# A hybrid decoder layer on one core: another order for the steps of a half's mix, and other PSUM banks for two units

## The chip, the cores and the metric

The kernel runs on one core of one Trainium2 chip. The metric is the device time of one execution in microseconds. Three runs of the kernel before gave 2166.95, 2167.82 and 2168.07 us; their median, 2167.82 us, is the time before.

The engines are TensorE (PE in the profile, its weight loads are PEld), VectorE (DVE), ScalarE (ACT), GpSimd (POOL) and SyncE (SP, which here issues DMAs). Matmul results go to PSUM, which has eight banks of 128 x 512 float32.

## The reference, cut to what matters

One layer of a decoder over 2048 tokens of width 1024 in float32. The input is normalised and projected; four heads of a gated linear recurrence (HGRN2) and eight heads of sliding-window attention with sinks run side by side; their outputs are concatenated, projected by `w_out` and added to the input. A gated MLP with a causal depthwise convolution and a last norm follow.

```python
u = rmsnorm(h, norm_mix_w[l])
proj = u @ w_in[l]
hq, hf, hi, hg, att = jnp.split(proj, [...], axis=-1)
f = lb + (1.0 - lb) * jax.nn.sigmoid(hf)          # forget gate, k = 1 - f
o_hg = hgrn2_chunkwise(q_hg, 1.0 - f, v_hg, jnp.log(f))
o_hg = rmsnorm(o_hg, hg_norm_w[l]) * jax.nn.silu(hg)
o_att = sliding_window_attention_with_sinks(aq, ak, av, sinks[l])
h = h + jnp.concatenate([o_hg, o_att], axis=-1) @ w_out[l]
v = rmsnorm(h, norm_ffn_w[l])
gate = causal_depthwise_conv(v @ w_gate[l], conv_w[l], conv_b[l])
h = h + (jax.nn.silu(gate) * (v @ w_up[l])) @ w_down[l]
```

## The kernel before

**Tiling.** Activations lie transposed: features on the 128 partitions, tokens along the free axis. The tokens are worked in two halves of 1024. Every float32 operand of a large product is split into a high and a low part of type fp32r (`split`, `prep`, lines 186 to 229: a copy on ScalarE and a subtraction on VectorE), and a product is three matmuls: high times high, high times low, low times high. The norm's scale of a token is applied when a result is read out of PSUM.

**A unit** (`unit`, line 195) is the product of a 1024 x 128 weight tile with the half's activations: eight input tiles (`X`, or the finished mix `M`) times three matmuls times two banks of 512 tokens, 48 matmuls into two banks. The weights come by DMA into one of three buffers and are split in a ring of two.

**PSUM.** Line 64 to 66 divide the eight banks: four `mm` for the units, and four side banks, two `hg` and two `at`. `kind="aux"` puts a unit's two results into one `hg` and one `at` bank.

**The mix of a half** (lines 1200 to 1238) works four recurrent heads and four pairs of attention heads. Both are Python generators that give back control between steps. `hgrn` (line 524) has five steps:

- 1: the units of the forget gate (`f`) and the query (`hq`), and their read-out;
- 2: products on the diagonal, then seven levels of doubling block size (`LEVELS`); a level copies operands on ScalarE (`G`, line 601), multiplies on TensorE (`plev`), scales `QK` by `F` on VectorE (line 615) and puts the block into `ST`; levels 2 to 16 send a part round by a small DMA on ScalarE's queue (line 582);
- 3: `pkn`, the state products `pu`, and the running states `SS`;
- 4: the output gate's unit `g`;
- 5: the products `po`, their norm, the transposition `pot`, and the gated output.

For the last head the gate's unit comes in step 2, after the diagonal, and the levels alone are step 3; `pu` is step 4 and the output step 5. `QK`, `f` and `SS` have one buffer each, so a head waits there for the one before it.

`attend` (line 431) has four steps: the query unit `q`; the scores `psc` of both token groups with their softmax; and the weighted sums of group 0 and of group 1 (`ppt` transposes, two masks on VectorE, `poT`).

The output of a head goes to `mix[h]`, of a pair to `mix[4 + j]`. The last head and the last pair write theirs split; the other six are split at lines 1214 and 1215, into the buffers of `X`, which come free as the last unit, the last head's gate, passes over them. `out_proj` (line 744) then runs eight units `pop` over the tiles of `M` in the order 0, 4, 1, 5, 2, 6, 7, 3. `BEHIND` (line 38) puts parts of its second and third unit behind marks of the last head: the third unit's first tile behind `pu`, its third behind `po`, its sixth behind `pot`.

**Between the halves.** `down` (line 1017) runs seven products (a Strassen scheme) over the four `mm` banks and the four side banks in turn. In the first half its last two are P2 in the side banks and P4 in `mm`; VectorE adds them to `hh` (lines 1137 to 1146). It then starts the next half: the keys' unit and the values' unit (`first_unit`, both in `mm`), among which two sums `pst` and their spreads `pinv` (lines 258 to 288) go through the side banks, and the forget gates of the first head, `f0`, in the side banks (lines 1185 to 1187). The first half gets the same three from `head` (line 314).

**What sets the order.** The framework plans the order of instructions ahead, with a simulated clock. The order of the program is the order of priority: each engine takes what is ready, by the simulation, and stands first in the program. So a unit that stands later in the program fills TensorE between the small products of earlier steps. `tc.issue_after` puts an instruction behind another on the same engine. On the chip each engine runs its planned list in order.

In each half, with H for `next` of a recurrent head, A of an attention pair, W and V for the values' weights and product, G for the early split of a gate's weights and S for the six splits, the order before is:

```
H0 A0 W H0 V G0 A0 H0 H0 A0 A0 H0
H1 H1 A1 G1 A1 H1 H1 A1 A1 H1
H2 H2 A2 G2 A2 H2 H2 A2 A2 H2
H3 A3 H3 S H3 A3 H3 A3 H3 A3
```

Of the kernel before, what the change touches and what calls it, by code (L numbers as in the profile page):

```python
# [19 lines left out]
KT = D // P  # L20
S = 2048
# [4 lines left out]
HG = 4  # L26
ATT_J = 4
# [16 lines left out]
WARM = 12  # L44
TAIL_WARM = 7
LV = 4


@with_exitstack
def hymba_layer(ctx: ExitStack, tc: tile.TileContext, a: dict, out: bass.AP):  # L50
    nc = tc.nc

    def pool(name, bufs=1, space=None, stack=ctx, **kw):
        if space is not None:
            kw["space"] = space
        return stack.enter_context(tc.tile_pool(name=name, bufs=bufs, **kw))
# [12 lines left out]
    def ps(kind, name):  # L69
        return spaces[kind].tile([P, 512], F32, tag=kind, name=name)  # L70

    aux = ("hg", "at")

    def halves():
        return [(b, slice(b * 512, (b + 1) * 512)) for b in range(NB)]
# [104 lines left out]
    def raw4(src):  # L180
        t = wp.tile([P, D], F32, tag="raw", name="raw", bufs=RAW)
        if src is not None:
            nc.sync.dma_start(t, src)
        return t

    def prep(src, slots=False):

        raw = raw4(src)
        hi, lo = [hp.tile([P, D], F32R, tag="m", name=f"w{t}", bufs=KT) if slots else
                  wp.tile([P, D], F32R, tag=t, name=f"w{t}", bufs=2) for t in ("hi", "lo")]  # L190
        nc.scalar.copy(hi, raw)  # L191
        nc.vector.tensor_tensor(lo, raw, hi.bitcast(F32), op=ALU.subtract)  # L192
        return hi, lo

    def unit(src, X, name, order=range(KT), kind="mm", then={}, behind={}, in_turn=False):


        hi, lo = src if isinstance(src, tuple) else prep(src)
        o = [ps(aux[b] if kind == "aux" else kind, f"{name}{b}") for b in range(NB)]
        order, mark = list(order), None  # L200
        for both in [[h] for h in halves()] if in_turn else [halves()]:
            for i, kt in enumerate(order):
                if i in then:
                    then[i]()
                wh, wl = hi[:, kt * P:(kt + 1) * P], lo[:, kt * P:(kt + 1) * P]
                xh, xl = X[kt]
                if i in behind:
                    mark = marks[behind[i]].ins
                with tc.issue_after(mark) if mark else ExitStack():
                    for w, x, f, l in ((wh, xh, kt == order[0], False), (wh, xl, False, False),  # L210
                                       (wl, xh, False, kt == order[-1])):
                        for b, bs in both:
                            marks["unit"] = nc.tensor.matmul(o[b], w, x[:, bs], start=f, stop=l)  # L213
        return o
# [5 lines left out]
    def split(src, w=None, eng=None, dst=None):  # L220

        h, l = dst or new_x()
        if w is None:
            nc.scalar.copy(h, src)
            (eng or nc.vector).tensor_tensor(l, src, h.bitcast(F32), op=ALU.subtract)
        else:
            nc.scalar.activation(h, src, AF.Identity, scale=w)
            nc.vector.scalar_tensor_tensor(l, src, w, h.bitcast(F32), op0=ALU.mult, op1=ALU.subtract)
        return h, l
# [161 lines left out]
            f0 = unit(F, X, "f", kind="aux", then={4: st.spread}, behind={4: "pinv"})  # L391
        return o, st.acc, st.rs, f0, summed

    def first_unit(X, i, then={}):
        return unit(a["w_att"][ATT_J + i], X, "kv", then=then)

    def rows(kv):
        return slice(kv * HD, (kv + 1) * HD)
# [125 lines left out]
    def hgrn(hf, h, X, invb, vs, WG, mix, p, fu=None):  # L524
# [51 lines left out]
        def place(m, pl):  # L576

            plv = pl.rearrange("p (r b c m) -> p r b c m", r=R, c=2, m=m)
            moved, odd = [p.tile([P, R, 64], F32, tag="lv", name=n, bufs=LV) for n in ("moved", "odd")]
            nc.scalar.copy(moved.rearrange("p r (b m) -> p r b m", m=m), plv[:, :, :, 1])  # L580
# [118 lines left out]
    def project_v(hf, parts, X, rs, p):  # L699

        v = p.tile([P, HG, TT, P], F32, name="v")
        for tt in range(TT):
            o = ps("mm", "pvv")
            t = slice(tt * P, (tt + 1) * P)
            for kt in range(KT):
                hi, lo = parts[kt // 2]
                xh, xl = X[kt]
                c = slice((kt % 2) * 512, (kt % 2 + 1) * 512)
                nc.tensor.matmul(o, xh[:, t], hi[:, c], start=kt == 0, stop=False)
                nc.tensor.matmul(o, xl[:, t], hi[:, c], start=False, stop=False)  # L710
                nc.tensor.matmul(o, xh[:, t], lo[:, c], start=False, stop=kt == KT - 1)
            nc.scalar.activation(v[:, :, tt], o.rearrange("p (h d) -> p h d", h=HG), AF.Identity,
                                 scale=rs[:, tt:tt + 1])
        return [v[:, h] for h in range(HG)]
# [302 lines left out]
    def down(hf, kept, acts, p):  # L1017
# [8 lines left out]
        S = {}  # L1026
# [78 lines left out]
        X, xs, acc = [], None, None  # L1105
        end = len(todo) - NP
        for k, (name, _, _, j) in enumerate(todo):
            if k + 2 < len(todo):
                ready[k + 2] = prep_piece(k + 2)
            if j == 0:  # L1110
# [4 lines left out]
                else:  # L1115
                    o = by if name == "P3" else bx
                if name == "P3":
                    acc = inv_tile() if final else wp.tile([P, HALF], F32, tag="raw", name="sums", bufs=RAW)
                    s1, s2 = [Stats(acc[:, bs], lambda: p.tile([P, 512], F32, tag="ut", name="fsq", bufs=UT))
                              for bs in (lo, hi)]  # L1120
# [3 lines left out]
            if not final and k >= end - 3:  # L1124
                xs = next(loading, xs)
# [29 lines left out]
        if final:  # L1155
# [26 lines left out]
            steps[1][0].inverse("o", last)  # L1182
            finish(hf, hh, steps[1][0], steps[1][1], [nc.scalar, nc.sync], steps[1][0].spread(1))
            return None
        kv = [first_unit(X, 0, {3: lambda: s1.inverse("o"), 7: lambda: xs.inverse("x")})]
        kv.append(first_unit(X, 1, {2: lambda: (s1.spread(), finish(hf, hh, s1, lo, [nc.sync])), 4: xs.spread}))
        f0 = unit(a["w_f"][0], X, "f", kind="aux")
        return X, kv, xs.acc, xs.rs, f0

    def finish(hf, hh, st, bs, queues, inv=None):  # L1190
        for d in range(KT):
            t = hh[d][:, bs]
            nc.vector.tensor_tensor(t, t, st.acc if inv is None else inv, op=ALU.mult)
            queues[d % len(queues)].dma_start(out[d, :, hf * HALF + bs.start:hf * HALF + bs.stop], t)

    X = []
    *nxt, summed = X, *head(X)
    for hf in range(NH):
        X, kv, invb, rs, f0 = nxt
        with ExitStack() as st:  # L1200
            p = pool(f"mix{hf}", stack=st, reuse_waits="tile")
            KS, V = att_keys(hf, kv, invb, p)
            mix = [None] * KT
            vs = []
            M, WG = {}, {}
            for h in range(HG):
                hg = hgrn(hf, h, X, invb, vs, WG, mix, p, f0 if h == 0 else None)
                at = attend(hf, h, X, invb, KS, V, mix, p)
                with tc.issue_after(summed.ins) if hf + h == 0 else ExitStack():
                    next(hg)  # L1210
                if h == HG - 1:
                    next(at)
                    next(hg)
                    for kt in (0, 4, 1, 5, 2, 6):
                        M[kt] = split(mix[kt])
                    next(hg)
                elif h == 0:
                    next(at)
                    wv = [prep(a["w_v"][s], s > 1) for s in range(4)]
                    next(hg)  # L1220
                    vs += project_v(hf, wv, X, rs, p)
                else:
                    next(hg)
                    next(at)
                if h < HG - 1:
                    WG[h] = prep(a["w_g"][h])
                next(at)
                next(hg)
                if h < HG - 1:
                    next(hg)  # L1230
                next(at)
                if h < HG - 1:
                    next(at)
                    next(hg)
                else:
                    next(hg)
                    next(at)
            M[7], M[3] = mix[7], mix[3]
        with ExitStack() as st:
            p = pool(f"ffn{hf}", stack=st, reuse_waits="tile")  # L1240
            kept, ops, hs, first, last = out_proj(hf, M, p)
            acts = gate_up(hf, ops, hs, first, last, p)
            nxt = down(hf, kept, acts, p)
# [61 lines left out]
```

## Time and profile before

| What | Value |
|---|---|
| median of three runs | 2167.82 us |
| profiled execution, its own time | 2166.65 us |
| its span | 2164.9 us |
| mean granted clock of TensorE over the span | 0.998 |
| VectorE busy, share of the span | 77% |
| ScalarE busy, share of the span | 50% |
| mean DMA traffic | 119 GB/s |

The span runs from the first instruction to the last; the execution's own time has 1.75 us around it. A row of a timeline or of the chain of waits begins with the start and the length in us; a row of groups ends with the busy time and the mean length in ns of one instruction, and then the idle time of the engine before them. A matmul's row is longer than its share of TensorE's time, since matmuls overlap: what counts is the distance from start to start.

### The profile page before, as it was taken

What the parts mean: (1) busy time and instruction counts of PE and PEld (TensorE: products, weight loads), DVE (VectorE), ACT (ScalarE), POOL (GpSimd) and SP (SyncE); (2) the same over time, 40 slices, a digit from 0 to 9 for tenths busy, and PEclk for the clock granted to TensorE, in tenths of its full rate; (3) what the DMA queues carried; (4) which work ended last, traced back from release to release, by engine and by line L of the source; (5) the groups of instructions that cost most, each with busy time, mean ns of one, the idle gap of its engine ahead of it and who ended that gap; (6) DMA issues with size and microseconds to landing.
All of it is one profiled execution on the core that took longest, in us unless ns stands there. A gap on an engine that the chain in (4) does not pass through costs nothing.

```text
span 2164.9 us, 28224 instructions
## 1 busy us (share of the span) xinstructions
PE 2142.5 (99%) x10752; PEld 1790.8 (83%) x10752; DVE 1658.0 (77%) x2446; ACT 1091.6 (50%) x1858; POOL 6.5 (0%) x28
## 2 busy tenths in 40 slices
PE   9999999999999999999999999999999999999998
PEld 7888888888888888888788888878888888888888
DVE  6557888798887878776864688877978888887766
ACT  6456566564444444435624476645544444454353
POOL 1000000000000000000000000000000000000000
PEclk9999999999999999999999999999999999999999
DMA  4111112413232335954631011214233323259643
GB/s 157 49 40 39 44 44 77 141 51 132 88 123 92 106 103 180 384 204 165 204 127 57 32 39 39 79 46 144 66 106 102 117 83 127 93 197 395 225 141 132
DMA packets 94383, 258.04 MB, mean 119 GB/s; under 512 B 11416, under 2 KB 17576, under 8 KB 94248
## 3 DMA queue, kind: packets, MB, share of 16 engines
q1 hardware_dynamic: 88992, 251.30, 33.9%
q10 hardware_dynamic: 5256, 4.94, 0.8%
q8 instruction: 84, 1.38, 0.3%
q14 instruction: 51, 0.42, 0.1%
HBM read 195.10 MB, written 57.15 MB: 117 GB/s over the span
## 4 chain that ended last, share of the span: by engine, by line
PE 93%; DVE 4%; ACT 1%; DMA 1%; issue 1%; SPq 0%; ACTq 0%; DVEq 0%
PE X L888 7%; PE X L889 7%; PE X L890 7%; PE pop L213 7%; PE hq L213 4%; PE f L213 4%; PE q L213 4%; PE Y L890 4%; PE Y L888 4%; PE Y L889 4%; PE g L213 4%; PE pdx L1099 3%; PE pdx L1101 3%; PE pdx L1100 3%; PE pdy L1101 2%; PE pdy L1100 2%
## 5 line engine op out<-in xcount | busy, mean ns | idle before, releaser
L717 ACT CAST whi<-raw 128x1024 fp32r<-128x1024 f32 x88 | 92.8, 1054 | 109.6 <-PE X L889 68.1
L888 PE MATMUL X<-T,whi 128*128 128x512 f32 x352 | 136.9, 389 | 0.0
L889 PE MATMUL X<-T,whi 128*128 128x512 f32 x352 | 136.9, 389 | 0.0
L890 PE MATMUL X<-T,wlo 128*128 128x512 f32 x352 | 136.9, 389 | 0.0
L983 DVE SCALAR_TENSOR_TENSOR y<-ga,cw,y 128x1024 f32<-128x1024 f32 x88 | 112.5, 1281 | 26.0 <-ACT y L981 26.0
L895 ACT COPY u<-X 128x512 f32<-128x512 f32 x88 | 51.6, 586 | 133.6 <-PE X L890 133.4
L191 ACT CAST whi<-raw 128x1024 fp32r<-128x1024 f32 x57 | 59.6, 1051 | 95.7 <-PE q L213 28.1
L718 DVE TENSOR_TENSOR wlo<-raw,whi 128x1024 fp32r<-128x1024 f32 x88 | 107.4, 1221 | 0.0
L192 DVE TENSOR_TENSOR wlo<-raw,whi 128x1024 fp32r<-128x1024 f32 x57 | 69.4, 1221 | 43.2 <-ACT whi L191 42.8
L718 DVE TENSOR_TENSOR xld<-raw,xhd 128x1024 fp32r<-128x1024 f32 x72 | 80.8, 1134 | 21.9 <-ACT xhd L717 21.4
L717 ACT CAST xhd<-raw 128x1024 fp32r<-128x1024 f32 x72 | 69.7, 979 | 44.8 <-DMA raw<-act0T 17.8
L213 PE MATMUL pop<-XH,whi 128*128 128x512 f32 x256 | 84.5, 394 | 0.9 <-ACT XH L520 0.8
L213 PE MATMUL pop<-XL,whi 128*128 128x512 f32 x256 | 85.3, 391 | 0.0
L213 PE MATMUL pop<-XH,wlo 128*128 128x512 f32 x256 | 84.4, 390 | 0.4 <-DVE wlo L192 0.4
L889 PEld LDWEIGHTS X<-T,whi 128*128 128x128 f32 x352 | 66.1, 188 | 13.7
L888 PEld LDWEIGHTS X<-T,whi 128*128 128x128 f32 x352 | 66.1, 188 | 13.7
L890 PEld LDWEIGHTS X<-T,wlo 128*128 128x128 f32 x352 | 66.1, 188 | 13.7
L1099 PE MATMUL pdx<-xhd,hid 128*128 128x512 f32 x192 | 74.4, 391 | 1.0 <-ACT hid L717 1.0
L1100 PE MATMUL pdx<-xld,hid 128*128 128x512 f32 x192 | 74.7, 389 | 0.0
L1101 PE MATMUL pdx<-xhd,lod 128*128 128x512 f32 x192 | 73.7, 389 | 0.0
L615 DVE TENSOR_TENSOR QK<-QK,f 128x1024 f32<-128x1024 f32 x56 | 68.5, 1223 | 4.8 <-ACT G L601 4.2
L888 PE MATMUL X<-T,Sh 128*128 128x512 f32 x176 | 68.7, 390 | 1.5 <-ACT s L895 1.5
(384 smaller groups left out, 6430.1 us busy)
## 6 DMA issues: line engine op xcount, KB each, us to landing
wr<-in_w_down SPq DMA_DIRECT2D x90, 512.0 KB, 5.8
raw<-in_w_gate SPq DMA_DIRECT2D x44, 512.0 KB, 3.6
raw<-in_w_up SPq DMA_DIRECT2D x44, 512.0 KB, 3.5
raw<-act0T SPq DMA_DIRECT2D x20, 512.0 KB, 8.2
raw<-act1T SPq DMA_DIRECT2D x20, 512.0 KB, 6.7
act0B<-y SPq DMA_DIRECT2D x33, 256.0 KB, 2.3
act1B<-y SPq DMA_DIRECT2D x33, 256.0 KB, 2.3
raw<-in_w_out SPq DMA_DIRECT2D x16, 512.0 KB, 7.4
```

Source lines behind the costliest of these rows:

```text
L192: nc.vector.tensor_tensor(lo, raw, hi.bitcast(F32), op=ALU.subtract)
L213: marks["unit"] = nc.tensor.matmul(o[b], w, x[:, bs], start=f, stop=l)
L615: done = nc.vector.tensor_tensor(own, own, Fv.rearrange("p b w -> p w b").unsqueeze(3).to_broadcast([P, 2, nb, m]), op=ALU.mult)
L717: return (nc.scalar.copy(h, src), (eng or nc.vector).tensor_tensor(l, src, h.bitcast(F32), op=ALU.subtract))
L718: (eng or nc.vector).tensor_tensor(l, src, h.bitcast(F32), op=ALU.subtract))
L888: nc.tensor.matmul(o, wh[:, ws], xh, start=i == 0 and not more, stop=False, skip_group_check=more)
L889: nc.tensor.matmul(o, wh[:, ws], xl, start=False, stop=False, skip_group_check=more)
L890: r = nc.tensor.matmul(o, wl[:, ws], xh, start=False, stop=i == 3, skip_group_check=more)
L983: nc.vector.scalar_tensor_tensor(y, g[:, w:w + HALF], C.cw[:, ft, w:w + 1], y, op0=ALU.mult, op1=ALU.add)
L1099: nc.tensor.matmul(o, wh[:, i, c], ah[:, i, cols], start=f, stop=False, skip_group_check=more)
L1100: nc.tensor.matmul(o, wh[:, i, c], al[:, i, cols], start=False, stop=False, skip_group_check=more)
L1101: nc.tensor.matmul(o, wl[:, i, c], ah[:, i, cols], start=False, stop=l, skip_group_check=more)
```

## The change

The order of the steps is now written out as a string, and a loop works through it.

```diff
+ORDER = """
+H0 A0 W0 H0 V0 G0 A0 H0 H0 A0 H0 H1 A0 H1 A1 G1 A1 H1 H1 A1 A1 H2 H1 H2 A2 G2 A2 H2 H2 A2 A2 H2 H3 A3 H3 H3 S A3 H3 A3 H3 A3
+"""
+SPLIT = (0, 4, 1, 5, 2, 6)
...
-    def first_unit(X, i, then={}):
-        return unit(a["w_att"][ATT_J + i], X, "kv", then=then)
+    def first_unit(X, i, then={}, kind="mm"):
+        return unit(a["w_att"][ATT_J + i], X, "kv", kind=kind, then=then)
...
-        kv = [first_unit(X, 0, {3: lambda: s1.inverse("o"), 7: lambda: xs.inverse("x")})]
+        kv = [first_unit(X, 0, {3: lambda: s1.inverse("o"), 7: lambda: xs.inverse("x")}, "aux")]
...
-        f0 = unit(a["w_f"][0], X, "f", kind="aux")
+        f0 = unit(a["w_f"][0], X, "f")
...
-            for h in range(HG):
-                hg = hgrn(hf, h, X, invb, vs, WG, mix, p, f0 if h == 0 else None)
-                at = attend(hf, h, X, invb, KS, V, mix, p)
...
+            heads = [hgrn(hf, h, X, invb, vs, WG, mix, p, f0 if h == 0 else None) for h in range(HG)]
+            pairs = [attend(hf, j, X, invb, KS, V, mix, p) for j in range(ATT_J)]
+            wv = {}
+            for n, step in enumerate(ORDER.split()):
+                i = int(step[1:] or 0)
+                if step[0] == "H":
+                    with tc.issue_after(summed.ins) if hf + n == 0 else ExitStack():
+                        next(heads[i])
+                elif step[0] == "A":
+                    next(pairs[i])
+                elif step[0] == "W":
+                    wv[i] = [prep(a["w_v"][s], s > 1) for s in range(4)]
+                elif step[0] == "V":
+                    vs += project_v(hf, wv[i], X, rs, p)
+                elif step[0] == "G":
+                    WG[i] = prep(a["w_g"][i])
+                else:
+                    for kt in SPLIT:
                         M[kt] = split(mix[kt])
...
-            M[7], M[3] = mix[7], mix[3]
+            for kt in range(KT):
+                M.setdefault(kt, mix[kt])
```

Against the order before, the order of three places differs in each half:

- head 0's output (its fifth H) and head 1's first units (the first H1) come before the last step of pair 0;
- head 2's first units (the first H2) come before head 1's output (the fifth H1);
- the last head's levels (the third H3) come before the six splits S.


Between the halves, the keys' unit goes into one `hg` and one `at` bank, and the first forget gates into two `mm` banks. The first half's keys, values and forget gates, which `head` makes, are left as they were. No instruction is added or taken away.

More of the change, by code (lines that the diff above doesn't have):

```diff
@@ L1205, in hymba_layer @@
             M, WG = {}, {}
-            for h in range(HG):
-                hg = hgrn(hf, h, X, invb, vs, WG, mix, p, f0 if h == 0 else None)
-                at = attend(hf, h, X, invb, KS, V, mix, p)
[L1209 to L1214, printed above, removed]
-                        M[kt] = split(mix[kt])
[L1216 to L1237, printed above, removed]
-            M[7], M[3] = mix[7], mix[3]
+            heads = [hgrn(hf, h, X, invb, vs, WG, mix, p, f0 if h == 0 else None) for h in range(HG)]
[16 more added lines that the diff above has]
+                    for kt in SPLIT:
+                        M[kt] = split(mix[kt])
+            for kt in range(KT):
+                M.setdefault(kt, mix[kt])
         with ExitStack() as st:
```

## The prediction

> **What bounds the kernel now.** I read the page first: the busy shares, then the chain of work that ended last.
>
> ```profile
> span 2164.9 us, 28224 instructions
> PE 2142.5 (99%) x10752; PEld 1790.8 (83%) x10752; DVE 1658.0 (77%) x2446; ACT 1091.6 (50%) x1858; POOL 6.5 (0%) x28
> PE 93%; DVE 4%; ACT 1%; DMA 1%; issue 1%; SPq 0%; ACTq 0%; DVEq 0%
> ```
>
> TensorE is idle for 2164.9 - 2142.5 = 22.4 us in all, and the change adds and removes no instruction. So it can only move idle time of TensorE: what other engines do counts where TensorE waits for them. Next I read TensorE's waits in three stretches, with the windows around them: the end of each half's mix, and the passage from the first half's down projection to the second half's first unit.
>
> ```profile
> PE plev L612 <- DVE ST L586: 1.8, 1, 1.8
> PE poT L509 <- DVE y L171: 1.4, 1, 1.4
> PE psc L460 <- DVE sc L469: 0.2, 1, 0.2
> ...
> PE plev L612 <- ACT G L601: 2.0, 2, 1.3
> PE ppt L496 <- DVE sc L469: 1.8, 1, 1.8
> PE pop L213 <- ACT XH L520: 0.8, 1, 0.8
> PE poT L509 <- DVE m L475: 0.6, 1, 0.6
> PE pop L213 <- DVE wlo L192: 0.4, 1, 0.4
> ...
> 325.40:350.40 25.00, 24.79 (x168) 21.40 (x166) 22.60 (x42) 20.41 (x44) 0.00 (x0) 1.00 0.43 138
> 350.40:373.90 23.50, 20.19 (x174) 17.68 (x175) 18.86 (x46) 10.65 (x45) 0.00 (x0) 1.00 0.02 6
> 1394.30:1420.00 25.70, 25.44 (x143) 21.93 (x141) 23.11 (x39) 20.44 (x44) 0.00 (x0) 1.00 0.45 142
> 1420.00:1435.00 15.00, 10.11 (x97) 8.40 (x97) 11.67 (x25) 9.07 (x30) 0.00 (x0) 0.77 0.09 25
> ```
>
> The first three waits (columns: total us, times, longest) lie between 340 and 380, the end of the first half's mix: 3.4 us. The next five lie between 1400 and 1470, the second half's: 5.6 us. The windows (busy us and count of PE, of its weight loads, DVE, ACT, POOL; then the granted clock and the DMA share) start where the last gate unit ends, 325.4 and 1394.3. TensorE then runs 25 us nearly full and runs dry after it. It is 15.00 - 10.11 = 4.9 us idle from 1420 to 1435, and there the granted clock averages 0.77; in the first half it stays at 1.00. VectorE is 90% busy in both 25 us windows: it is what TensorE waits for.
>
> Why it is 25 us:
>
> ```profile
> L213 PE MATMUL pop<-XH,whi 128*128 128x512 f32 x24 | 8.3, 399 | 0.0
> ...
> L213 PE MATMUL pop<-XH,whi 128*128 128x512 f32 x24 | 7.6, 391 | 0.0
> ...
> 356.14 2.01 PE pu L656 x16
> ...
> 1435.71 1.81 PE pu L656 x16
> ```
>
> The first two rows are groups of the two 25 us windows: 24 is a third of 72 matmuls, that is two units of the output projection with six of their eight tiles each. Their seventh tile is att3 and the eighth the last head's output, and the third unit is put behind `pu`, the state products of the last head. `pu` starts 30.7 us after the gate's end in the first half and 41.4 us in the second. Time that the last head's levels gain is therefore time that TensorE gains, until the gap is closed.
>
> **The change, part by part.**
>
> *Banks.* The passage between the halves (matmuls, VectorE, matmuls):
>
> ```profile
> 1074.09 0.39 PE L1101 MATMUL pdx<-xh2d,gad 128*128 128x512 f32 x1
> ...
> 1075.01 0.68 DVE L1085 TENSOR_TENSOR h<-h,pdx 128x512 f32<-128x512 f32 x1
> ...
> 1075.84 0.47 PE L213 MATMUL kv<-XH,whi 128*128 128x512 f32 x1 [1.37 <-DVE y L177]
> ...
> 1104.15 10.88 PE f L213 x48
> ```
>
> A unit of 48 matmuls takes 10.88 us, so matmuls start every 0.227 us. The keys' first matmul could start at 1074.09 + 0.227 = 1074.32, and starts at 1075.84: its bank is one of the four that the last product leaves to VectorE, whose first add ends at 1075.69. In the side banks nothing holds it: product P2 was read out of them when P4 began, 4 x 33 matmuls or 30 us earlier. **-1.5 us**; bounds 0 (another input late) and -1.5. The forget gates follow 28 us later in the unit banks that P4's third and fourth output used; nothing waits there.
>
> What it adds: the keys hold one of the two `hg` banks until they are read out, so two sums and two spreads queue for the other one.
>
> ```profile
> 1087.49 1.84 PE L267 MATMUL pst<-ones,invb 128*128 128x1 f32 x16
> ...
> 1088.13 0.16 DVE L165 TENSOR_SCALAR ms<-pst 128x4 f32<-128x4 f32 x1
> ```
>
> The second sum now starts at 1087.49, before VectorE has read the first at 1088.13 to 1088.29. With one bank it starts 0.8 us later. Behind it on TensorE stand matmuls of the keys' and values' units; whoever needs the sum, the keys' read-out, has the 10.88 us forget unit as cover. Cost between 0 (units go first) and +0.8 us (TensorE stands); I take 0, the row's cover.
>
> *Moved steps in the middle.* Head 1's forget and query units now come before A0's last step, head 2's before head 1's output.
>
> ```profile
> 159.61 5.94 PE hq L213 x26
> 165.55 1.90 PE poT L509 x32
> ...
> 225.49 1.68 PE poT L509 x28
> 227.17 0.42 PE po L674 x2
> ...
> 229.59 1.39 PE hq L213 x6
> 230.98 0.44 PE ppt L496 x4
> 231.41 0.94 PE hq L213 x4
> ```
>
> In the chain, A0's last step puts 1.90 us of `poT` and 0.44 us of `ppt` into head 1's query unit: without them it ends 2.3 us earlier. Head 2's query unit has ten matmuls left (1.39 + 0.94 = 2.3 us) after head 1's `po`; put first, they delay `po` by 2.3 us, and with it the buffer QK and the banks that head 2 needs. I take the two as cancelling: 0. Bounds: -2.3, and +10.9 per half if a whole unit stood ahead of `po`. TensorE is busy without a break through the first half's mix, past the last gate's end:
>
> ```profile
> 31.00:350.00 319.00, 319.00 (x1909) 271.05 (x1907) 228.62 (x422) 187.08 (x405) 0.00 (x0) 1.00 0.17 51
> ```
>
> So an order costs nothing there but what it does to the last head. The loads keep their order on SP's queue: the steps that were passed issue none.
>
> *Levels before splits.* For the last head the six splits of finished outputs come behind the seven levels. They issue no DMA; the levels issue four small ones on ScalarE's queue, as now.
>
> ```profile
> 325.40 1.22 DVE L225 TENSOR_TENSOR XL<-hg,XH 128x1024 fp32r<-128x1024 f32 x1
> ...
> 328.33 1.22 DVE L225 TENSOR_TENSOR XL<-att,XH 128x1024 fp32r<-128x1024 f32 x1
> 329.46 1.23 DVE L615 TENSOR_TENSOR QK<-QK,f 128x1024 f32<-128x1024 f32 x1
> 330.60 1.22 DVE L192 TENSOR_TENSOR wlo<-raw,whi 128x1024 fp32r<-128x1024 f32 x1
> ...
> 1402.88 1.22 DVE L225 TENSOR_TENSOR XL<-hg,XH 128x1024 fp32r<-128x1024 f32 x1
> ...
> 1404.62 1.22 DVE L225 TENSOR_TENSOR XL<-att,XH 128x1024 fp32r<-128x1024 f32 x1
> ...
> 1406.35 1.23 DVE L615 TENSOR_TENSOR QK<-QK,f 128x1024 f32<-128x1024 f32 x1
> ```
>
> The second level's product (L615) starts at 329.46; two of the splits on VectorE between 325 and 330, ahead of it, are 2.4 us. In the second half two splits, 2.4 us less a small overlap, stand before it: 2.3 us. In the first half 2.4 us covers the waits for `psc` and `plev`, 0.2 + 1.8 = 2.0 us: **-2.0 us** (the 1.4 us for `poT` hangs on the attention, which doesn't get earlier). In the second half 4.9 us of idle is left after 1420, so all 2.3 us count: **-2.3 us**. Bounds: from 0, should the attention's steps only take the freed slots, to all the waits, -3.4 and -5.6. The delayed splits have cover: the first four are done before the gate ends, and the fifth is needed 4 x 1.36 us after it (six matmuls a tile).
>
> *Clock.* From 1420 to 1435 the granted clock averages 0.77 with no single wait over 1.8 us. [...] What a full clock would bring on top is in the low end of the range only.
>
> **Sum.** -1.5 - 2.0 - 2.3 = -5.8 us. The profiled execution took 2166.65 us, 1.75 more than its span, and so would take 2160.9. The median before, 2167.82, lies 1.17 above it: I forecast **2162.0 us**, with 2158.5 to 2165.5 as its own range. 0.2% of the time, 4.3 us, is about what a measurement can tell from no change.
>
> **Rivals.**
> 1. *Only the banks pay.* VectorE is 90% busy in the 25 us windows, so scores and weight splits (wlo at 330.60) may fill what the splits leave, and `pu` comes as late as now. For it: the work of VectorE up to the end is the same in any order. Against: the chain through the levels is what ends last there. 2167.8 - 1.5 = 2166.3. This is also the case that the step order does not take effect as written, since each engine's order is planned from priorities.
> 2. *The ends close altogether.* The second half's last head is late because its predecessor was: `pu` comes 10.7 us later after the gate than in the first half, by the same program. A new order may undo that. Then all the waits go: -1.5 - 3.4 - 5.6 = -10.5, and the `poT` at half clock give up to 1.4 more: 2155.9 to 2157.3; I say 2156.5.
> 3. *Slower: head 1's output is held back.* The place is TensorE at 223 and its like in the second half: two units of 10.9 us now rank before `po`, QK and the `hg` banks stay taken, and heads 2 and 3 start late. At the end each us late is a us of idle, since the 25 us of cover are used up. 2.3 us a half is what the rows show; to be slower by 4.3 us it takes (5.8 + 4.3) / 2 = 5.1 us a half, which is half a unit still ahead of `po`. With 8 us, between that and the bound of 10.9: 2162.0 + 16 = 2178.
>
> **How the numbers follow.** Forecast 0.49, banks only 0.26, ends closed 0.13, held back 0.12. Of the forecast's 0.49, 0.40 lies below 2163.5. Faster: 0.40 + 0.13 = 0.53. Within 0.2%: 0.09 + 0.26 = 0.35. Slower 0.12. The range leaves out most of the held-back case and the lowest edge: 2155.5 to 2169.
>
> **What would show it.** Right: `kv` starts about 0.23 us after the last `pdx`; the last head's L615 has at most one split before its second product; `pu` starts less than 30 us after the gate's end in the first half and less than 40 in the second; TensorE's waits there fall to some 1.4 and 3.3 us. Wrong: a new wait of `pop` for `XL` or `wlo` right after the gate (the splits had no cover); `pu` later than now (held back); a wait in the middle of the mix, where there is none; a wait of `pst` or `pinv` near 1088 (the shared bank).

## The result, and the profile after

The change takes **2161.82 us** (median of nine runs, 2160.15 to 2163.34) where the kernel before takes 2167.82 (2166.64 to 2169.08): ratio 0.9973, 95% interval 0.9964 to 0.9981. The forecast was 2162.0. Of its 5.8 us of gain, though, 4.3 were put down to an edit that did nothing. The ratios here and below leave out two executions, one of e3 (3617 us) and one of the kernel before (3080 us), in which the mean granted clock was 0.56 and 0.65.

The page of the kernel after (its span, the busy shares, the chain of work that ended last):

```profile
span 2161.4 us, 28224 instructions
...
PE 2139.3 (99%) x10752; PEld 1788.9 (83%) x10752; DVE 1660.8 (77%) x2446; ACT 1091.7 (51%) x1858; POOL 6.0 (0%) x28
...
PE 95%; DVE 2%; ACT 1%; DMA 1%; issue 1%; SPq 0%; DVEq 0%; ACTq 0%
```

TensorE's share of the chain went from 93% to 95%; the other engines did the same work. The passage between the halves, as TensorE's timeline has it:

```profile
1076.91 0.39 PE L1105 MATMUL pdx<-xh2d,gad 128*128 128x512 f32 x1
1077.14 0.39 PE L217 MATMUL kv<-XH,whi 128*128 128x512 f32 x1
```

The keys' first matmul follows the last of the down projection by 0.23 us, where it had been 1.75. TensorE's waits at the ends of the two mixes (total us, times, longest), the first two rows from 320 to 380, the others from 1380 to 1480:

```profile
PE plev L616 <- DVE ST L590: 2.9, 1, 2.9
PE poT L513 <- DVE y L175: 1.4, 1, 1.4
...
PE poT L513 <- DVE y L175: 1.4, 1, 1.4
PE plev L616 <- ACT G L605: 1.2, 1, 1.2
PE ppt L500 <- DVE sc L473: 1.0, 1, 1.0
PE pkn L653 <- ACT ST L639: 0.3, 1, 0.3
PE pu L660 <- ACT Kn L654: 0.2, 1, 0.2
```

The first half's waits **grew** from 3.4 to 4.3 us; the second half's fell from 5.6 to 4.1, and the waits of the output projection (`pop`) are gone. The windows of the two ends (length, busy time of PE, its weight loads, DVE, ACT and POOL, then the granted clock):

```profile
350.10:373.60 23.50, 19.26 (x154) 17.46 (x154) 18.84 (x47) 10.98 (x45) 0.00 (x0) 0.85 0.02 6
...
1420.00:1435.00 15.00, 12.23 (x133) 10.75 (x128) 12.14 (x29) 10.95 (x46) 0.00 (x0) 1.00 0.03 9
```

The clock changed places: 0.85 in the first half, where it had been 1.00, and 1.00 in the second, where it had been 0.77. From the starts of the same matmuls in both traces, the whole time by stages:

| from one matmul to the next named | before | after | difference |
|---|---|---|---|
| start to the last gate unit's end (`g`), first half | 325.15 | 324.85 | -0.3 |
| to the last of the output projection (`pop`) | 114.19 | 117.33 | **+3.1** |
| to the last of the down projection (`pdx`) | 634.74 | 634.74 | 0 |
| to the first of the keys (`kv`) | 1.75 | 0.23 | **-1.5** |
| to the last gate unit's end, second half | 318.22 | 319.13 | +0.9 |
| to the last of the output projection | 121.99 | 115.09 | **-6.9** |
| to the last of the down projection | 638.39 | 639.61 | +1.2 |
| to the end | 10.45 | 10.46 | 0 |

That is -3.5 us for these two executions (spans 2164.9 and 2161.4). The one of before was among its shortest, the one of after among its longest; the medians differ by 6.0. The +1.2 belongs to the one execution: in e12, the same program once more, that stage takes 638.43. So in these two executions the order of the steps gained 6.0 us in the second half (+0.9 - 6.9) and lost 2.8 in the first. The two rows of the second half count only together: 12 matmuls (eight `pot`, four `pdiag`) stand behind the gate's end before and ahead of it after. From the keys' first matmul to the last `pop` it is 440.2 us before and 434.2 after.

### The profile page after: what moved, and what is told of

It is laid out like the page before. It is cut to its first block, busy times and chain, and to the rows that moved or that the text cites. A ratio compares the mean times of both kernels' runs of the same rounds, so it can differ in the third digit from the quotient of the medians.

```text
span 2161.4 us, 28224 instructions
## 1 busy us (share of the span) xinstructions
PE 2139.3 (99%) x10752; PEld 1788.9 (83%) x10752; DVE 1660.8 (77%) x2446; ACT 1091.7 (51%) x1858; POOL 6.0 (0%) x28
## 4 chain that ended last, share of the span: by engine, by line
PE 95%; DVE 2%; ACT 1%; DMA 1%; issue 1%; SPq 0%; DVEq 0%; ACTq 0%
PE X L892 7%; PE X L893 7%; PE X L894 7%; PE pop L217 7%; PE f L217 4%; PE q L217 4%; PE hq L217 4%; PE pdx L1103 4%; PE pdx L1105 4%; PE Y L894 4%; PE Y L893 4%; PE pdx L1104 4%; PE Y L892 4%; PE g L217 4%; PE pdy L1104 3%; PE pdy L1105 3%
```

## The experiments

Two readings stood against each other. The **prediction's**: the last head's levels gain what the splits no longer take, and the moved steps in the middle cancel. The **rival**, read from the trace after: the levels gained nothing (their products stand where they stood in the first half), and the time came from where the moved steps put head 2's output. "Gate to `pu`" is the distance from the last gate unit's end to the last head's state products, the prediction's measure: 30.7 and 41.3 us before, 33.4 and 31.4 after.

| run | kept of the change | ratio to before, 95% interval | gate to `pu`, first and second half |
|---|---|---|---|
| the change | all | 0.9973 (0.9964 to 0.9981) | 33.4, 31.4 |
| e1 | banks | 0.9989 (0.9980 to 0.9998) | 32.1, 41.2 |
| e2 | levels first | 0.9998 (0.9989 to 1.0006) | 30.7, 41.2 |
| e3 | head 1's move | 1.0005 (0.9996 to 1.0013) | 34.5, 35.5 |
| e4 | head 2's move | 1.0004 (0.9995 to 1.0013) | 32.8, 41.2 |
| e5 | banks, and an edge on VectorE | 1.0002 (0.9993 to 1.0011) | 30.7, 41.7 |
| e6 | banks, levels first put in force for two splits | 1.0010 (1.0001 to 1.0019) | 30.8, 42.9 |
| e7 | banks, new order in the second half only | 0.9965 (0.9953 to 0.9978) | 30.7, 31.4 |
| e8 | banks, head 1's move, levels first | 1.0007 (0.9998 to 1.0016) | 35.3, 35.4 |
| e9 | banks, and an edge on TensorE | 0.9979 (0.9970 to 0.9988) | 30.7, 31.4 |
| e10 | e7 and the edge of e9 | 0.9968 (0.9955 to 0.9980) | 30.7, 31.2 |
| e11 | e7 once more | 0.9966 (0.9953 to 0.9978) | 32.3, 31.4 |
| e12 | the change once more | 0.9969 (0.9957 to 0.9980) | 32.7, 32.1 |

### One part alone: e1 to e4

Each has before's order and banks but for one part. e1 has the two lines of the banks:

```diff
-        kv = [first_unit(X, 0, {3: lambda: s1.inverse("o"), 7: lambda: xs.inverse("x")})]
+        kv = [first_unit(X, 0, {3: lambda: s1.inverse("o"), 7: lambda: xs.inverse("x")}, "aux")]
-        f0 = unit(a["w_f"][0], X, "f", kind="aux")
+        f0 = unit(a["w_f"][0], X, "f")
```

> Before with the new banks alone (keys' unit in the side banks, first forget gates in the units' banks), the old order of steps. Both theories: the keys' first matmul starts about 0.23 us after the last pdx (before: 1.75 us after it), the wait on VectorE's y there is gone, and nothing else moves: -1.5 us, 2166.3. Were the whole gain of the change made by the banks, it would be 2162.

2166.76 us against 2168.25: **-1.5** (by the interval, -0.4 to -4.3), as both expected, with `kv` 0.23 us after the last `pdx`. e2 moves S behind the levels:

```diff
-H3 A3 H3 S H3 A3
+H3 A3 H3 H3 S A3
```

> Before with one edit: the six splits of the last head's finished outputs come behind its seven levels. The prediction's step: the last head's pu comes 2.0 us earlier in the first half (before: 30.7 us after the gate's end) and 2.3 us earlier in the second (41.4), 2163.5. Rival, read from the trace of after: the levels are held by TensorE's pdiag product and its bank, not by the splits, so that pu moves by under 0.5 us in both halves: 2167.8.

No difference, and there could be none: the instructions of e2 stand in the same order as before's on all five engines. In the plan each engine takes what is ready. Likely the second level's product isn't ready, in the plan's simulated time, when the splits are, so they go first wherever they stand in the program; the plan's times themselves are not shown. e2 is thus a second sample of before, and it corrects e1: with the old banks its `kv` comes 0.23 us after `pdx`, with no wait. What the banks remove is a wait that some executions have (`kv` comes 1.75 us after `pdx` in before's trace, 1.03 in e4's) and others don't (0.23 in e2's and in e3's).

e3 and e4 make the two other moves, one each:

```diff
-H0 H0 A0 A0 H0 H1 H1 A1
+H0 H0 A0 H0 H1 A0 H1 A1
```

```diff
-A1 A1 H1 H2 H2 A2
+A1 A1 H2 H1 H2 A2
```

> Before with one edit: head 1's forget and query units come before the first pair's last attention step. The prediction's step: up to -2.3 us with the middle's bound, without a counterpart to cancel it: 2165.5 to 2167.8. Rival: there is no wait of TensorE in the middle and what comes earlier there meets the same last head, 2167.8; only if the second half's 10 us of delay ahead of the last head (pu 41.4 us after the gate's end against 30.7) goes with this edit, 2163.

> Before with one edit: head 2's first step, with its forget and query units, comes before head 1's output. The prediction's step: the output is held back by 2.3 us in each half, and the last head with it, 2167.8 to 2172.4. Rival, read from the trace of after: this is the edit that costs the first half some 3 us (po 3 us later, a longer wait at its end with the clock halved) and lets the second half's head 2 run as in the first half, where its pu is then about 31 us after the gate's end instead of 41.4 (-5): about 2166 together.

Both 0. In e3 two effects cancel: the stage from the gate's end to the last `pop` takes 119.35 us in the first half (before: 114.19) and 119.18 in the second (121.99). e4 changes the order around head 1's output and nowhere else, so the last head's stays as it was; the rival's expectation for it was wrong in both halves. Yet the change has three moves, one of them is void, and two that bring nothing alone in the whole time bring its second half 6 us. In e3's trace the second half does gain: from the keys' first matmul to the last `pop` it takes 437.6 us, 2.7 less than before.

### Is it VectorE's order? e5

In before's second half the normalization of head 2's output waits behind three splits and a weight split (the expectation counts two of these; the other one comes behind it). e5 puts the splits behind it, in the old order:

```diff
+            marks["on"] = nc.vector.tensor_tensor(on[:, 4 * b:4 * b + 4], po[b]...
...
+                    with tc.issue_after(marks["on"].ins):
                         for kt in SPLIT:
                             M[kt] = split(mix[kt])
```

> Old order of steps with the new banks, and one ordering edge: VectorE's part of the six splits of finished outputs stands behind head 2's normalization (on<-po,y). Nothing is moved from its step. In before that normalization starts 14.2 us after head 2's last po in the second half (1378.3 to 1392.5, with three of the splits and two weight splits ahead of it) and 309.5 in the first half, ahead of all splits; the first half should not change. If the second half's late end comes from VectorE's order at this one place: pu about 31 to 35 us after the gate's end there (before: 41.4) and 2161 to 2163. If it comes from head 2's units standing late on TensorE, as the moved steps would have it: pu stays over 39 us after the gate's end, 2166.3.

`pu` stays at 41.7 us after the gate. The normalization now starts right behind its own scale, 6.8 us ahead of the gate's end instead of 1.8. The transposition behind it does come earlier too, 1.3 us ahead of the gate's end (1395.3 to 1396.6) instead of 3.3 behind it, but the diagonal products of the last head gain 0.9 us by it (6.4 behind the gate's end instead of 7.3) and `pu` nothing. So the splits' place in VectorE's order is not the cause.

### The levels ahead of the splits, in force: e6

e6 has the old order with the new banks and the levels written ahead of S, and an edge for the last two of the six splits, the two that stood between the gate's end and the second level's product:

```diff
+            if m == 2:
+                marks["two"] = done
...
                     for kt in SPLIT:
-                        M[kt] = split(mix[kt])
+                        with tc.issue_after(marks["two"].ins) if kt in (2, 6) else ExitStack():
+                            M[kt] = split(mix[kt])
```

> Old order with the new banks and the levels written ahead of the splits, and an ordering edge that makes it count: VectorE's part of the last two splits (head 2's output, the third pair's) stands behind the second level's product. The prediction's step, now in force: pu 2 us earlier in each half (before: 30.7 and 41.4 us after the gate's end), 2162.3 with the banks. Rival: level 2 waits for ScalarE's copy G, which waits for a buffer of pdiag's product, so the product moves by 1.1 us at most and the output projection's seventh tile may come late: pu within 1 us of before in the first half, 2165 to 2167.

Now these two splits do stand behind the second product. VectorE's timeline of e6 in the first half, and ScalarE's:

```profile
327.56 1.21 DVE L619 TENSOR_TENSOR QK<-QK,f 128x1024 f32<-128x1024 f32 x1
328.70 1.21 DVE L229 TENSOR_TENSOR XL<-hg,XH 128x1024 fp32r<-128x1024 f32 x1
329.83 1.22 DVE L229 TENSOR_TENSOR XL<-att,XH 128x1024 fp32r<-128x1024 f32 x1
...
330.96 1.22 DVE L196 TENSOR_TENSOR wlo<-raw,whi 128x1024 fp32r<-128x1024 f32 x1
...
333.89 1.28 DVE L571 TENSOR_TENSOR hg<-hg,g 128x512 f32<-128x512 f32 x2
...
336.18 1.27 DVE L619 TENSOR_TENSOR QK<-QK,f 128x1024 f32<-128x1024 f32 x1
```

```profile
331.37 1.12 ACT L570 ACTIVATE g<-hg 128x512 f32<-128x512 f32 x2
332.43 1.04 ACT L605 COPY G<-QK 128x1024 f32<-128x1024 f32 x1
```

The second level's product is at 327.56, before at 329.46: 1.9 us gained, with the gate's end at 325.7 instead of 325.4 even 2.2. The third is at 336.18, before at 335.83: relative to the gate's end nothing is left. VectorE works without a break there: in both kernels the same 10.4 us of its work lie between the gate's end and the third product, the two splits among them. The edge only moved the two from ahead of the second product to ahead of the third. Also ahead of the third, in both kernels, stand the gate's sigmoid on ScalarE (331.37; before 331.05), the next operand copy `G` behind it (332.43; before 332.11), and VectorE's gate product behind the sigmoid (333.89; before 333.01). These hang on the gate and not on the splits; how much they alone would leave to gain isn't shown, since no run has all six splits behind the seven levels. What e6 shows is that a second product 2.2 us earlier is worth nothing to `pu`, which comes 30.8 us after the gate. In the second half the second product comes 1.9 us earlier against the gate and `pu`, 42.9 us after it, does not; there the clock is at half for 10.2 us (before: 6.8). The run was a little slower than before.

### Where head 2's output stands: e7 to e10

Putting the traces side by side gave a second theory. `QK` has one buffer, which head 2's `po` reads last; the last head's chain begins when it is free. From the end of `po` to the last head's `pu` it takes 54.7 to 60.1 us in every run, in whatever order. By this theory TensorE's work behind `po` is what fills that time, and **each us that `po` gains against the last gate unit's end brings `pu` about a us nearer to that end**. The windows of before, from `po` to the gate's end and from there to `pu`, first half and second half:

```profile
299.40:325.40 26.00, 26.00 (x144) 21.43 (x143) 23.02 (x39) 15.70 (x28) 0.00 (x0) 1.00 0.21 66
325.40:356.10 30.70, 28.56 (x195) 24.54 (x194) 28.30 (x50) 23.73 (x52) 0.00 (x0) 1.00 0.36 116
...
1377.00:1394.30 17.30, 17.30 (x79) 14.31 (x79) 16.74 (x31) 13.54 (x25) 0.00 (x0) 1.00 0.13 41
1394.30:1435.60 41.30, 36.15 (x242) 30.73 (x241) 35.38 (x63) 30.12 (x74) 0.00 (x0) 0.92 0.31 98
```

And of the change:

```profile
302.50:325.10 22.60, 22.60 (x129) 18.61 (x128) 21.25 (x36) 15.60 (x27) 0.00 (x0) 1.00 0.16 49
325.10:358.50 33.40, 30.53 (x195) 26.75 (x193) 29.86 (x52) 24.20 (x53) 0.00 (x0) 0.91 0.34 108
...
1373.20:1396.50 23.30, 23.30 (x132) 19.22 (x131) 21.42 (x36) 15.74 (x27) 0.00 (x0) 1.00 0.16 51
1396.50:1427.90 31.40, 28.63 (x196) 24.26 (x194) 28.28 (x50) 24.23 (x54) 0.00 (x0) 1.00 0.34 114
```

In each pair the lengths add up to 56.7 and 58.6 us before, 56.0 and 54.7 after. In the second half `po` ends 23.3 us ahead of the gate's end instead of 17.3; in the first, 22.6 instead of 26.0. Why it was late in before's second half, on TensorE:

```profile
1369.55 0.38 PE L674 MATMUL po<-v,ST 128*128 128x128 f32 x2
...
1374.81 0.44 PE L509 MATMUL poT<-pp,V 128*64 128x128 f32 x4
...
1376.71 0.49 PE L675 MATMUL po<-SS,QK 128*128 128x128 f32 x2
```

`po` starts at 1369.55, is cut by six matmuls of the query unit, and its last two wait behind 32 of the attention's `poT`. From head 2's `pu` (1361.5) to the end of `po` it is 15.5 us here and 9.6 in the first half. Read this way, e3 and e8 fit as well: `po` ends 20.7 and 20.3 us ahead of the gate there, and gate to `pu` is 34.5 to 35.5 in either half.

e7 gives each half its better order, by `ORDER[hf]` with before's string for the first half:

```diff
-            for n, step in enumerate(ORDER.split()):
+            for n, step in enumerate(ORDER[hf].split()):
```

> New banks; the first half in the old order of steps, the second half in the new. If the new order costs the first half its end (po 3 us later, a wait of 2.9 us for the level products instead of 1.8) and pays only in the second: pu 30.7 to 32.5 us after the gate's end in both halves, first half's end as in before, 1 to 3 us faster than the change: 2159 to 2161. If the two halves hang together, or the first half's loss is the clock's alone and not the order's: as the change, 2161.8.

2160.72 us, with 114.21 us from the gate's end to the last `pop` in the first half, as before (the change: 117.33), and 115.10 in the second, as the change. So the second half's gain doesn't need the first half's new order. The first half's loss goes with the new order by way of the clock: its wait of 2.9 us (2.8 in e12), where the old order has 1.8, was followed by half clock in both profiled executions of the change (0.50 from 352.55 to 359.38; in e12 a mean of 0.83 from 350 to 360), and that accounts for most of the 3.1 us; the old order met half clock there in three of ten. e8 is the change without head 2's move:

> The change without one of its moves: head 1's output stands before head 2's units again. With head 1's move alone, the first half's pu came 34.5 us after the gate's end and the second half's 35.5; with all moves 33.4 and 31.4. If head 2's move is needed for the gain: pu 35 us after the gate's end in both halves, 2165 to 2167. If head 1's move makes the gain and head 2's costs 2.3 us a half, as the prediction had it: 2158 to 2160.

2169.58 us: head 2's move is needed for the gain, where the prediction had it as a cost. The time is above what was expected. In the profiled execution the clock was at half for 10.2 us at the first half's end and 6.8 at the second's; in e3's for 3.4 and 6.8. Apart from the banks e8 and e3 have TensorE's instructions in the same order, since the levels' place is void here too, and with the new banks e8 is no faster (1.0007 against 1.0005).

e9 tests the theory with no step moved. The old order gets one edge on TensorE:

```diff
-        o = unit(a["w_att"][j], X, "q")
+        o = unit(a["w_att"][j], X, "q", behind={0: "po"} if j == 3 else {})
```

> Old order of steps with the new banks, no step moved, and one ordering edge on TensorE: the query unit of the fourth pair stands behind head 2's po. In all runs so far the last head's pu starts 54.7 to 60 us after the end of head 2's po, and the gate ends 26.0 us after it in before's first half, 17.3 in its second, 23.3 in the second half of the change. If po's place on TensorE is the cause: po ends 21 to 24 us before the gate's end in the second half, pu comes 32 to 36 us after the gate (before: 41.3), and the time is 2161 to 2163.5, as with the change. If what counts is that the moved steps bring attention and heads nearer to each other: pu stays at 41, 2166.3. If TensorE stands before po instead, for want of the query unit's matmuls: the end is shorter, a wait of po of as much is new, 2166.3.

TensorE's timeline of e9 around the end of `po`, and the windows from there to the gate's end and on to `pu`:

```profile
1369.55 0.44 PE L513 MATMUL poT<-pp,V 128*64 128x128 f32 x4 [2.45 <-DVE pp L503]
...
1373.11 0.39 PE L679 MATMUL po<-SS,QK 128*128 128x128 f32 x2
1373.25 0.71 PE L217 MATMUL q<-XH,whi 128*128 128x512 f32 x2
```

```profile
1373.30:1397.00 23.70, 23.70 (x111) 19.68 (x111) 21.45 (x36) 15.19 (x26) 0.00 (x0) 1.00 0.18 52
1397.00:1428.40 31.40, 28.63 (x196) 24.27 (x194) 28.27 (x50) 24.23 (x54) 0.00 (x0) 1.00 0.34 112
```

`po` ends 23.7 us ahead of the gate's end and `pu` comes 31.4 us after it, to a tenth as in the change. The stage to the last `pop` takes 115.11 us (the change: 115.09, before: 121.99), with the same 12 matmuls moved ahead of the gate. For the length of that stage, the place of head 2's `po` on TensorE is the cause, shown. The edge has its price: the wait of 2.45 us in the first row, and a stage from the keys to the gate's end of 322.3 us where the change has 319.1. So of the 6.4 us that `po` gains against the gate here, 2.3 are `po` earlier and 4.1 the gate later; in the change it is 5.1 and 0.9. From the keys' first matmul to the last `pop` e9 takes 437.4 us: 2.8 of the change's 6.0 us, and the 2.45 us of waiting are most of what is missing. At 2164.54 us, above the 2161 to 2163.5 expected, e9 lies between the banks alone and the change, and by the intervals it is separated from neither.

e10 adds the edge to e7:

> First half in the old order, second half in the new, new banks, and the same edge: the fourth pair's query unit behind head 2's po (this moves 11 matmuls, 2.5 us, behind po in the second half and none in the first). If each us that po gains is a us at the end: pu 29 us after the gate's end in the second half instead of 31.4, 2158.3. If TensorE now waits at po for its operands as long as the 11 matmuls took: 2160.7, with the wait moved there.

`po` ends 25.8 us ahead of the gate's end, and `pu` still comes 31.2 us after it; 2161.38 us. TensorE has a new wait there:

```profile
PE psc L466 <- DVE sc L475: 1.4, 1, 1.4
```

The rule ends there: beyond some 23 us it is other work behind the gate that ends last, such as these scores on VectorE. Before's first half, with 26.0, stands at 30.7 too.

### Beside each other on one chip: e11 and e12

> First half in the old order, second half in the new, new banks, once more, beside the change on one chip: 2160.7, 1 to 2 us faster than the change.

> The change itself once more, beside the others on one chip: 2161.8. Its first half's end should take 0 to 3.4 us from one execution to the next by whether the granted clock falls to 0.5 after the 2.9 us wait, with the same order of work.

2161.16 us (2159.56 to 2161.89) and 2161.98 (2159.89 to 2162.78). The version with an order for each half is 0.8 us faster by the medians here and 1.1 in the first pair of runs, which these runs don't separate from nothing. The traces fit a small difference: the first half's loss is 3.1 us where the clock falls for 6.8 us, 2.0 in e12 where it falls for 3.4, and e11 lost 1.6 us to the clock in its old order.

## Why the prediction was right, and where it was not

- **TensorE bounds, only its idle time can move.** Right. It was incomplete: behind some of the idle time the clock stood at 0.50, and that time counts too (last section).
- **Banks, -1.5.** Right in place and kind. The size is right for an execution with the full wait, as the one that the prediction was read from (1.75 to 0.23 us); of the four traces with the old banks two have no such wait and one has half of it, some 0.6 us in the mean, and the times (e1; e8 beside e3) don't fix the size. No wait of `pst` or `pinv` showed: the shared bank cost nothing, as taken.
- **Levels before splits, -2.0 and -2.3.** This step failed. The edit changes no engine's order (e2), so both terms were 0, and with two splits put behind the second product by force nothing is gained either (e6). The step went by the splits that stood ahead of the second product, and didn't ask what held the third. Rival 1 named both: that the order may not take effect as written, and that other work of VectorE may fill what the splits leave, with `pu` as late as before. The signs named beforehand showed it: all six splits still stand ahead of the second product, `pu` came 33.4 us after the gate in the first half, not under 30, and TensorE's waits are 4.3 and 4.1 us, not 1.4 and 3.3.
- **Moved steps in the middle, 0.** This failed too, and covered the other. The rule it went by, that an order costs nothing there but what it does to the last head, was right; the price was not. The two moves do not cancel but work together on head 2's `po`: 6.0 us forward in the second half, 3.4 us back in the first. That is rival 2's mechanism (the second half's last head is late because its predecessor was) in one half, and rival 3's (an output held back) in the other. For rival 2 the prediction had the number, 41.4 against 30.7 us by the same program, and gave it 0.13; its size, all waits gone, didn't come.
- **Clock: waits at their own length, a full clock in the low end only.** Too small on both sides. No run shows that waits always cost their own length and no more; the traces show 1.67 to 2.22 us of idle within 3.41 us and a clock of 0.50 behind it (last section). An estimate from the start-to-start distances of TensorE's matmuls, at half clock against full clock for the same kinds: the half clock cost about 3 us in before's second half (6.8 us at half) and nothing after; in the first half nothing before and about 3 us after (6.8 us at half). Of the 6.0 us gained in the second half 1.4 are then shorter waits (5.5 to 4.1 us) and about 3 the clock; the rest, some 1.5 us, is closer spacing of the matmuls at full clock.

The sum, -5.8, met -6.0 by luck: the second half gained more than both failed terms together, by a move that the prediction had as a cost, and the first half gave part of it back.

What stays open: why the plan cuts head 2's `po` in before's second half and not in its first. Both have the same order of steps. The plan's simulated times may differ there, which no run shows. Open too are what spaces the matmuls closer in the change's second half, and what splits behind all seven levels would bring.

## What to carry to other kernels

Where one buffer hands work from one stage to the next (here `QK`), follow the chain from the instruction that frees it to the one that TensorE runs dry for; count what TensorE has behind that instruction, and move by that count, up to the point where other work ends last. Before an order of steps is priced, see whether the planned order of any engine changes at all. And price one half, or one iteration, at a time: one string of steps gained 6 us in one half and lost 3 in the other.

## What the runs showed of the hardware

The granted clock fell to half behind waits of less than 3 us. Windows of e1, which has before's instructions in this half in the same order, of the change, and of before:

```profile
349.24:352.66 3.42, 1.75 (x30) 1.30 (x24) 2.92 (x6) 2.55 (x8) 0.00 (x0) 1.00 0.06 17
352.66:356.07 3.41, 3.02 (x14) 3.02 (x15) 2.51 (x7) 1.46 (x4) 0.00 (x0) 0.50 0.05 17
```

```profile
349.14:352.55 3.41, 1.19 (x6) 0.62 (x4) 2.47 (x4) 2.57 (x9) 0.00 (x0) 1.00 0.02 6
352.55:355.97 3.42, 2.77 (x13) 2.77 (x14) 2.72 (x6) 1.37 (x4) 0.00 (x0) 0.50 0.09 27
```

```profile
351.30:354.71 3.41, 1.77 (x16) 1.77 (x16) 3.41 (x7) 1.40 (x5) 0.00 (x0) 1.00 0.11 34
354.71:358.13 3.42, 3.34 (x29) 2.78 (x27) 3.42 (x10) 2.10 (x5) 0.00 (x0) 1.00 0.00 0
```

Between the first 100 us and the last ten, the trace of before has half clock from 1423.09 and from 1429.91, 3.41 us each, and the change's has it from 352.55, for 6.83 us. In the 3.41 us ahead of each of these TensorE was idle for 2.19, 1.86 and 2.22 us, in e1's for 1.67. In before's first half 1.64 us of idle, the last two windows above, were followed by a clock of 1.00. Why 1.67 us was followed by half clock and 1.64 was not is not shown.

The same wait of 1.8 us in the old order's first half had a lower clock behind it in some executions and not in others: from 350 to 360 the mean clock was 0.83 in e1 and e11, and 1.00 in e7, e9 and e10. Of the ten profiled executions with that order there, the stage from the gate's end to the last `pop` took 114.2 to 114.3 us in the seven that kept the clock and 115.6 to 116.3, 1.4 to 2.1 us more, in the three that had half clock for 3.4 us. The spread between executions goes with it: of the 77 runs of before that stood beside e1 to e12, the median is 2165.1 us at a mean granted clock of 0.999 (3 runs), 2167.3 at 0.998 (27), 2168.7 at 0.997 (33), 2169.0 at 0.996 (10) and 2170.8 at 0.995 (4).
